# The input projection of a hybrid encoder layer: pairs of blocks by Strassen's seven products

## The chip, the cores and the metric

The kernel runs on one core of one Trainium2 chip. The metric is the device time of one execution in microseconds (us); lower is better. A core has five engines that work side by side, each through its own instructions in the order in which they are written: TensorE (PE, matmuls and weight loads), VectorE (DVE), ScalarE (ACT), GpSimd (POOL) and SyncE (SP, which here issues DMAs). Matmuls add up in PSUM, eight banks of 128 x 512 fp32; everything else lies in SBUF or in DRAM.

## The reference

One layer for 768 tokens (512 of a prompt, 256 of a sample) of width 2048, in fp32. The input projection is the largest product, and the change is made to it:

```python
hn = rmsnorm(h, norm_g[i])
proj = hn @ w_in[i]                      # (768, 2048) @ (2048, 10240)
s_x, s_z, q, k, v, a_z, g_s, g_a = jnp.split(proj, cuts, axis=-1)
# widths 1024, 1024, 1024, 1024, 1024, 1024, 2048, 2048
y = s5_direction(u, ..., False) + s5_direction(u, ..., True) + ssm_d * u      # u is s_x in 64 groups of 16
y = gelu(y); y = y * sigmoid(y @ glu_w + glu_b); y = y * silu(s_z); y_s = y @ w_branch_s
o = diff_attention(q, k, v, rel_bias, lam)                                    # 4 heads, two softmaxes each
y_a = (rmsnorm(o, subln_g) * (1 - lam_init) * silu(a_z)) @ w_branch_a
merged = sigmoid(g_s) * y_s + sigmoid(g_a) * y_a
h = h + merged @ w_out                   # then the per-layer input's gate (2048 x 2048) and the last norm
```

## The kernel before

**Products.** Every fp32 operand of a large product is split in two parts (`split`, L93): ACT copies it to the high part, DVE subtracts that to get the low part. A product is then three matmuls: low by high, high by low, high by high. `Feat` (L211) makes 128 output columns feature-major: 128 x 128 weights are stationary, 384 tokens move, and the two token halves have a bank each. With K = 2048 a block has 16 k-tiles, so 16 x 3 x 2 = 96 matmuls of 384 columns, and its weights come in two pieces of 128 x 1024. `Tok` (L263) makes v token-major with 256 moving columns. Of `w_in`, 72 blocks go through `Feat`: 8 for s_x, 8 each for s_z, q, k and a_z, 16 each for the gates g_s and g_a.

**Weights.** `wload` (L180) loads piece after piece by SP into three buffers, `wsplit` (L189) splits each two pieces ahead; `ahead` (L1395) calls both. The accumulators rotate over four banks in this phase, two for each block, so a block's sums have the time of the next block to leave them; the other four banks are the side work's.

**Order.** `run_blocks` (L1402) walks the pieces, each in two halves of 24 matmuls. A half is a slot: `slot_e` (L105) first issues stores that have come due (`later`, L102) and lets each side lane issue its next piece for ACT, DVE and DMA; after the half's matmuls `slot_p` (L114) lets it issue matmuls. The side work is a queue of generators, which yield twice for each slot. The blocks come as: the projection of p while x comes in (`x_gen`, L346, splits x times the norm's gain); s_x, s_z, a_z, g_s, eleven blocks of g_a; then for each head v, k, q; the last five blocks of g_a. Beside them runs `s5_all` (L875): parameters, then for each half of the groups (`s5_half`, L597) nine batches of the inputs in five slots each, a scan over chunks (L795), four DVE operations a step and three steps a slot, and nine slots of outputs; then the gelu in nine slots. `attention` (L997) runs beside the next head's blocks. `drain` (L1435) runs what the lanes still hold when the blocks are done.

**Results.** `ev_silu` (L408) and `ev_gate` (L417) multiply by the norm's scale R, apply the sigmoid and store to DRAM; k, q and v (`ev_qk`, L956; `ev_v`, L949) go split into the attention's tiles. `y_prep` (L1133) loads and splits y for the GLU in four slots; `o_prep` (L1194), `ev_ds` (L1211) and `ev_da` (L1225) use what was stored.

## Time and profile before

| | us |
|---|---|
| median of 3 runs (lowest, highest) | 2488.8 (2487.98, 2488.87) |
| span of the profiled execution | 2485.5 |
| PE busy, weight loads | 2451.7, 2426.7 |
| DVE, ACT, POOL busy | 1139.0, 735.1, 68.0 |

The profile is taken in one execution; its span runs from the first to the last instruction, and the median of the runs is 3.3 us above it. The page's first part gives the busy time of each engine, the windows give the same by stage with the granted TensorE clock (1.00 is full speed), the groups by form give the mean time of one instruction of one shape, and the waits tell which engine stood idle until what. The mean of a matmul in the groups contains the wait for the one ahead of it, so the time of one is read from a long row of them in the chain.

### The profile page before, as it was taken

Reading aid. Unit: us, or ns where it says so; the run is one execution under the profiler, and the core shown is the slowest. Engines: PE = TensorE matmul, PEld = TensorE weight load, DVE = VectorE, ACT = ScalarE, POOL = GpSimd, SP = SyncE. Lnnn points to the kernel's source line nnn. Section 1 sums busy time; section 2 is a strip of 40 time slices with the busy share of each in tenths; the row PEclk is TensorE's granted clock in tenths of the full one; section 3 lists DMA queues with packets and bytes.
Section 4 is the critical chain, followed back from the end, with each engine's and each line's share of the span. In section 5 each row is a group of like instructions: output and inputs, shape, how many; then the busy total and the mean of one; then the engine's idle time right before and its main releaser. Section 6 shows DMA issues by size and latency. Waiting matters only on the chain.

```text
span 2485.5 us, 35850 instructions
## 1 busy us (share of the span) xinstructions
PE 2451.7 (99%) x14902; PEld 2426.7 (98%) x14902; DVE 1139.0 (46%) x2281; ACT 735.1 (30%) x1300; POOL 68.0 (3%) x58
## 2 busy tenths in 40 slices
PE   7999999999999999999999999999999999999997
PEld 7999999999999999999999999999999999999986
DVE  8645648535556627123343434452345232253346
ACT  5223321323231233123232323431123221133233
POOL 5000000000000000000000000000000000000003
PEclk9999999999999999999999999999999999999998
DMA  7262322473222467222222122553332322222234
GB/s 293 85 157 96 110 85 87 140 158 112 92 94 94 120 173 271 79 60 64 68 65 69 56 72 73 196 182 111 104 119 98 93 86 92 80 89 86 82 115 163
DMA packets 118051, 277.93 MB, mean 112 GB/s; under 512 B 28864, under 2 KB 47040, under 8 KB 117888
## 3 DMA queue, kind: packets, MB, share of 16 engines
q1 hardware_dynamic: 117312, 274.59, 35.5%
q8 instruction: 117, 1.92, 0.3%
q10 hardware_dynamic: 576, 1.05, 0.1%
q14 instruction: 46, 0.38, 0.0%
HBM read 216.94 MB, written 58.65 MB: 111 GB/s over the span
## 4 chain that ended last, share of the span: by engine, by line
PE 96%; DVE 1%; issue 1%; DMA 1%; POOL 1%; ACT 0%; SPq 0%; POOLq 0%; ACTq 0%; DVEq 0%
PE acc L83 88%; PE yps L83 2%; PE o L83 1%; PE vps L83 1%; PE s L83 1%; PE kps L83 1%; POOL y L1343 1%; DVE a L80 1%; PE wps L763 1%; DMA xr<-in_xT 1%; PE wt L1053 0%; PE bb L83 0%; DVE wl L72 0%; PE ot L1086 0%; DVE pps L389 0%
## 5 line engine op out<-in xcount | busy, mean ns | idle before, releaser
L83 PE MATMUL acc<-a,wh 128*128 128x384 f32 (+2 forms) x6912 | 1486.9, 335 | 0.0
L83 PEld LDWEIGHTS acc<-a,wh 128*128 128x128 f32 x6912 | 1224.4, 188 | 4.9
L83 PE MATMUL acc<-a,wl 128*128 128x384 f32 (+2 forms) x3456 | 898.4, 337 | 9.3 <-DVE wl L72 6.5
L83 PEld LDWEIGHTS acc<-a,wl 128*128 128x128 f32 x3456 | 619.4, 188 | 15.8 <-DVE wl L72 6.7
L72 DVE TENSOR_TENSOR wl<-raw,wh 128x1024 fp32r<-128x1024 f32 (+1 forms) x279 | 344.9, 1237 | 607.7 <-ACT wh L69 606.5
L69 ACT ACTIVATE wh<-raw 128x1024 fp32r<-128x1024 f32 (+1 forms) x279 | 292.7, 1051 | 605.9 <-PE acc L83 335.3
L83 PE MATMUL acc<-y,wh 128*128 128x384 f32 (+2 forms) x1024 | 222.6, 336 | 0.0
L72 DVE TENSOR_TENSOR stg<-acc,R 128x384 f32<-128x384 f32 (+2 forms) x160 | 86.4, 583 | 254.8 <-PE acc L83 254.7
L83 PEld LDWEIGHTS acc<-y,wh 128*128 128x128 f32 x1024 | 181.6, 189 | 1.8
L83 PE MATMUL acc<-wh,a 128*128 128x256 f32 x768 | 139.0, 283 | 0.0
L83 PE MATMUL acc<-y,wl 128*128 128x384 f32 (+2 forms) x512 | 134.0, 336 | 0.0
L83 PEld LDWEIGHTS acc<-wh,a 128*128 128x128 f32 x768 | 119.5, 191 | 0.3
L69 ACT ACTIVATE stg<-stg 128x384 f32<-128x384 f32 (+3 forms) x91 | 46.9, 542 | 240.7 <-DVE stg L72 240.7
L83 PE MATMUL acc<-wl,a 128*128 128x256 f32 x384 | 109.1, 284 | 0.0
L83 PEld LDWEIGHTS acc<-y,wl 128*128 128x128 f32 x512 | 93.3, 189 | 0.9
L69 ACT ACTIVATE stg<-y 128x384 f32<-128x384 f32 (+2 forms) x64 | 32.0, 525 | 160.2 <-DVE y L72 160.2
L83 PEld LDWEIGHTS acc<-wl,a 128*128 128x128 f32 x384 | 73.5, 191 | 0.2
L72 DVE TENSOR_TENSOR y<-acc,stg 128x384 f32<-128x384 f32 x32 | 16.4, 553 | 86.8 <-PE acc L83 86.8
L72 DVE TENSOR_TENSOR a<-acc,stg 128x384 f32<-128x384 f32 x32 | 16.4, 553 | 82.8 <-PE acc L83 82.8
L148 POOL TENSOR_TENSOR ors<-rsm,mhalf 128x1 f32<-128x1 f32 x24 | 13.0, 543 | 1487.5 <-DVE rsm L77 1487.5
L69 ACT ACTIVATE a<-stg 128x384 fp32r<-128x384 f32 (+1 forms) x48 | 26.2, 577 | 84.4 <-DVE stg L72 76.8
L69 ACT ACTIVATE st<-vps 64x252 f32<-64x252 f32 (+1 forms) x128 | 41.1, 321 | 20.8 <-PE vps L83 18.3
(223 smaller groups left out, 1730.2 us busy)
## 6 DMA issues: line engine op xcount, KB each, us to landing
raw<-in_w_in SPq DMA_DIRECT2D x144, 512.0 KB, 3.7
raw<-in_ple_g_w SPq DMA_DIRECT2D x42, 512.0 KB, 3.6
raw<-in_w_out SPq DMA_DIRECT2D x32, 512.0 KB, 3.6
d_q<-q SPq DMA_DIRECT2D x16, 512.0 KB, 3.8
q<-d_q SPq DMA_DIRECT2D x16, 512.0 KB, 3.8
raw<-in_w_v SPq DMA_DIRECT2D x16, 512.0 KB, 3.7
raw<-in_w_s SPq DMA_DIRECT2D x16, 512.0 KB, 3.7
raw<-in_w_a SPq DMA_DIRECT2D x16, 512.0 KB, 3.6
```

Of the source, the lines that this page charges most:

```text
L69: return nc.scalar.activation(out=out, in_=in_, func=func, **kw)
L72: return nc.vector.tensor_tensor(out=out, in0=a, in1=b, op=op)
L80: return nc.vector.scalar_tensor_tensor(out=out, in0=a, scalar=s, in1=b, op0=op0, op1=op1)
L83: return nc.tensor.matmul(out, lhsT, rhs, start=start, stop=stop, **kw)
L148: nc.gpsimd.tensor_tensor(out=out, in0=m, in1=mhalf[:, :ss.shape[1]], op=ALU.pow)
L763: nc.tensor.transpose(wps[x][:, g * 128:(g + 1) * 128], w[:, x, g], ident)
L1343: (nc.gpsimd if b % 3 else nc.vector).tensor_tensor(out=h, in0=h, in1=rb, op=M)
```

## The change

62 of the 64 blocks of s_z, q, k, a_z, g_s and g_a are taken in 31 pairs. K is gone through twice: first its rows 0 to 1023 for all pairs, then the others. Within a half of K the pair of blocks, the two quarters of K and the two token halves form a 2 x 2 by 2 x 2 product, made with seven products of 12 matmuls (4 k-tiles, 3 each) in place of eight (Strassen's scheme, in Winograd's form). Sums of weight tiles are made by DVE and split for each pair and half (`step`); sums of token tiles once for each half of K (`t_prep`, from x loaded again). The seven products go to three of four banks, and a bank is copied out by ACT or added by DVE one product later (`events`). Results of the first half are stored to DRAM without norm or activation; those of the second half are added there by a DMA of POOL's queue with `accum_op`. Two blocks of g_a go plainly, in parts of half of K, between the passes.

What follows from it elsewhere: the norm's scale and the activations come where the stored rows are used (gelu, `o_prep`, `ld_gate`, attention); v, k, q pass through DRAM and `attention` loads and splits them (21 slots a head, 18 before); s_x is stored in the order in which the groups are read; half the copies of the states for the outputs move from DVE to ACT; x's second half of K is loaded again between the passes; y is loaded and split at the last pair; silu and sigmoid are no longer applied on the way out.

```diff
+    def store(dst, st, add):
+        if add:
+            nc.gpsimd.dma_start(out=dst, in_=st, accum_op=A_)
+        else:
+            dma(dst, st)
+    class Quad:
...
+        def step(self, n, j):
+            r1, r2 = raws[j], raws[j + 1] if j + 1 in raws else None
+            lo, hi = slice(0, 512), slice(512, 1024)
...
+            if n == 0:
+                h, l = wtile("wh"), wtile("wl")
+                split(h, l, r1)
+                w["a11"], w["a12"] = (h[:, lo], l[:, lo]), (h[:, hi], l[:, hi])
+            elif n == 1:
+                u = wtile("wa", qpool["p"])
+                split(u[:, lo], u[:, hi], r2[:, hi])
+                w["a22"] = u[:, lo], u[:, hi]
+                tt(r2[:, hi], r2[:, lo], r2[:, hi], A_)
+            elif n == 2:
+                tt(r2[:, lo], r2[:, lo], r1[:, lo], A_)
+                tt(r1[:, lo], r1[:, lo], r2[:, hi], A_)
+            elif n == 3:
+                h, l = wtile("wh"), wtile("wl")
+                split(h, l, r2)
+                w["s3"], w["s1"] = (h[:, lo], l[:, lo]), (h[:, hi], l[:, hi])
+            elif n == 4:
+                u = wtile("wh")
+                split(u[:, lo], u[:, hi], r1[:, lo])
+                w["s2"] = u[:, lo], u[:, hi]
+            elif n == 5:
+                tt(r1[:, hi], r1[:, lo], r1[:, hi], A_)
+                u = wtile("wl")
+                split(u[:, lo], u[:, hi], r1[:, hi])
+                w["s4"] = u[:, lo], u[:, hi]
+                raws.pop(j), raws.pop(j + 1)
...
+        def product(self, n):
...
+            acc, wn, mov, k0, cols, first = ((self.A, "a11", None, 0, t1, 1), (self.B, "a12", None, 4, t1, 1),
+                                             (self.A, "s2", "u", 0, t1, 0), (self.C, "s3", "v", 0, t2, 1),
+                                             (self.A, "s1", "u", 0, t2, 0), (self.C, "a22", "v", 0, t1, 0),
+                                             (self.A, "s4", None, 4, t2, 0))[n]
...
+            if n == 0:
+                def f():
+                    self.o1 = stg()
+                    act(self.o1[:, lo], self.A)
+                e(1, f)
+            elif n == 1:
+                e(1, lambda: tt(self.o1[:, lo], self.o1[:, lo], self.B, A_))
+            elif n == 2:
+                def f():
+                    self.o2 = stg()
+                    act(self.o2[:, lo], self.A)
+                e(1, f)
+            elif n == 3:
+                e(1, lambda: act(self.o1[:, hi], self.C))
+            elif n == 4:
+                e(1, lambda: act(self.o2[:, hi], self.A))
+            elif n == 5:
+                def f():
+                    tt(self.o2[:, hi], self.o1[:, hi], self.o2[:, hi], S_)
+                    tt(self.o2[:, lo], self.C, self.o2[:, lo], S_)
+                e(1, f)
+                e(2, lambda: store(self.dsts[1], self.o2, self.half))
+            else:
+                e(1, lambda: act(self.o1[:, hi], self.A))
+                e(2, lambda: store(self.dsts[0], self.o1, self.half))
...
+    def t_prep(p):
...
+            if i < 4:
+                tt(b[:, HT:], a[:, HT:], b[:, HT:], S_)
+                tt(a[:, HT:], a[:, :HT], a[:, HT:], S_)
+                tt(a[:, :HT], b[:, HT:], a[:, :HT], S_)
+                tt(b[:, :HT], b[:, :HT], a[:, :HT], A_)
...
-                        nc.vector.tensor_copy(out=sb[64:128, :, x, c0:c0 + n], in_=v[64:128, :, ::-1])
+                        act(sb[64:128, :, x, c0:c0 + n], v[64:128, :, ::-1])
...
+                tt(z, z, R, M)
+                act(p, z, AF.Sigmoid)
                 tt(z, z, yn, M)
+                tt(z, z, p, M)
...
     def attention(h):
...
+        open_att()
+        vr = atile("vr", (128, NT, 256), F32)
+        dma(vr.rearrange("p t e -> p (t e)"), dv[h])
...
+        ld("k", dk)
...
+        vh, vl = atile("vh", (128, NT, 256)), atile("vl", (128, NT, 256))
+        split(vh, vl, vr)
...
+                if n == "q":
+                    stt(f, f, 128.0 ** -0.5, R, M, M)
+                else:
+                    tt(f, f, R, M)
+                split(hi, l, f)
...
     def run_blocks(lo, hi):
...
+            if isinstance(blk, Quad):
+                nxt = pieces[j + 2][0] if quad_of(j + 2) else None
+                blk.begin()
+                for n in range(7):
+                    prod[0] += 1
+                    hook(j, n)
+                    run_events()
+                    if n == 0:
+                        for k in range(blk.ready, 6):
+                            blk.step(k, j)
+                    elif n in (1, 6):
+                        if n == 6 and nxt:
+                            nxt.step(4, j + 2)
+                        more()
+                    elif nxt:
+                        nxt.step(n - 2, j + 2)
+                    elif n in (2, 5):
+                        wsplit(j + 2 + (n == 5))
+                    if prod[0] % 2 == 0:
+                        slot_e()
+                    blk.product(n)
+                    if prod[0] % 2 == 1:
+                        slot_p()
...
+    hooks[j - 2, 5] = [y_load]
+    hooks[j - 2, 6] = [lambda: y_split(range(4))]
+    hooks[j, 0] = [lambda: y_split(range(4, 8))]
```

## Rows read from the trace of the kernel before

**Rows 1.** The page's first part: busy us (share of the span) xinstructions.
```profile
PE 2451.7 (99%) x14902; PEld 2426.7 (98%) x14902; DVE 1139.0 (46%) x2281; ACT 735.1 (30%) x1300; POOL 68.0 (3%) x58
```

**Rows 2.** Windows: stretch, length, busy us (xcount) of PE, PEld, DVE, ACT, POOL, clock, DMA, GB/s.
```profile
16.00:60.00 44.00, 36.18 (x193) 34.81 (x192) 44.00 (x41) 26.60 (x39) 29.14 (x14) 0.96 0.75 278
367.50:471.50 104.00, 104.00 (x603) 104.00 (x602) 82.78 (x297) 22.02 (x33) 0.00 (x0) 1.00 0.33 105
755.00:859.00 104.00, 104.00 (x603) 104.00 (x602) 74.92 (x283) 20.21 (x30) 0.00 (x0) 1.00 0.35 101
921.50:960.00 38.50, 38.50 (x224) 38.50 (x223) 27.11 (x29) 15.63 (x20) 0.00 (x0) 1.00 0.73 252
1595.50:2080.00 484.50, 484.50 (x2797) 484.37 (x2796) 190.36 (x276) 115.05 (x160) 0.00 (x0) 1.00 0.36 120
```

**Rows 3.** The chain in order of time, 1600 to 1700 us: start, us, what, xcount.
```profile
1599.94 100.19 PE acc L83 x578
```

**Rows 4.** Waits, 14 to 64 us: who waited for whom, us, times, longest.
```profile
PE acc L83 <- DVE pps L389: 7.8, 4, 2.6
```

**Rows 5.** Groups by form, whole span: instruction, shapes, xcount, busy us, mean ns, idle before.
```profile
L72 DVE TENSOR_TENSOR wl<-raw,wh 128x1024 fp32r<-128x1024 f32 x277 | 343.5, 1241 | 604.7 <-ACT wh L69 603.5 <-DMA tp<-d_z 1.2
...
L72 DVE TENSOR_TENSOR w<-t,t 128x512 f32<-128x512 f32 x32 | 22.1, 692 | 1.1
...
L72 DVE TENSOR_TENSOR stg<-stg 128x384 f32<-128x384 f32 x38 | 19.5, 554 | 18.3 <-ACT stg L69 18.3
...
L72 DVE TENSOR_TENSOR y<-y,y 128x768 fp32r<-128x768 f32 x8 | 7.7, 959 | 7.3 <-ACT y L69 7.3
...
L69 ACT ACTIVATE wh<-raw 128x1024 fp32r<-128x1024 f32 x277 | 291.5, 1054 | 604.8 <-PE acc L83 335.3 <-issue 268.0 <-DMA raw<-in_ple_p 1.1
...
L69 ACT ACTIVATE stg<-y 128x512 f32<-128x512 f32 x5 | 3.2, 632 | 7.4 <-DVE y L72 7.4
...
L69 ACT ACTIVATE pps<-acc 128x384 f32<-128x384 f32 x16 | 7.2, 480 | 0.9 <-PE acc L83 0.9
...
L69 ACT ACTIVATE y<-y 128x768 fp32r<-128x768 f32 x8 | 6.8, 847 | 17.3 <-DVE y L72 17.3
```

**Rows 6.** Groups by form, DVE, the first scan's window, 367.5 to 471.5 us.
```profile
L72 DVE TENSOR_TENSOR st<-s,s 128x128 f32<-128x128 f32 x31 | 9.1, 292 | 1.1
...
L72 DVE TENSOR_TENSOR s<-s,st 128x128 f32<-128x128 f32 x31 | 8.8, 284 | 0.0
L72 DVE TENSOR_TENSOR st<-s,s 128x64 f32<-128x64 f32 x32 | 7.2, 225 | 1.1
...
L72 DVE TENSOR_TENSOR s<-s,st 128x64 f32<-128x64 f32 x32 | 7.0, 218 | 0.0
```

**Rows 7.** Groups by form, whole span: the gelu's DVE operations.
```profile
L72 DVE TENSOR_TENSOR yn<-y,p 128x768 f32<-128x768 f32 x8 | 14.1, 1768 | 0.0
...
L77 DVE TENSOR_SCALAR p<-p 128x768 f32<-128x768 f32 x8 | 4.4, 556 | 3.6 <-ACT p L69 3.5
```

**Rows 8.** DMA issues: out, in, queue, xcount, KB of one, median us to landing.
```profile
xr<-in_xT SPq DMA_DIRECT2D x8, 768.0 KB, 8.1
...
d_gs<-stg SPq DMA_DIRECT2D x16, 384.0 KB, 2.3
...
d_ysz<-z SPq DMA_DIRECT2D x8, 384.0 KB, 4.9
...
stg<-d_y SPq DMA_DIRECT2D x8, 384.0 KB, 3.6
```

**Rows 9.** Groups by form, whole span: ACT's copies of the states for the outputs.
```profile
L69 ACT ACTIVATE sb<-st 64x256 f32<-64x256 f32 x32 | 19.3, 653 | 0.0
...
L69 ACT ACTIVATE sb<-st 64x128 f32<-64x128 f32 x32 | 11.9, 420 | 0.0
```

**Rows 10.** Groups by form, 16 to 60 us: a busy POOL, and DVE beside it.
```profile
L356 POOL TENSOR_TENSOR sqa<-sqa,sq 128x768 f32<-128x768 f32 x7 | 17.9, 2550 | 0.6
...
L72 DVE TENSOR_TENSOR wl<-raw,wh 128x1024 fp32r<-128x1024 f32 x4 | 6.4, 1602 | 0.0
```

More of the change, by code (lines that the diff above doesn't have):

```diff
@@ L263, in _build, with __init__ @@
     class Tok:
-        def __init__(self, wname, first, xs, evac):
-            self.pieces = [d[wname][first + i] for i in range(4)]
-            self.xs, self.evac = xs, evac
+        def __init__(self, wname, first, xs, evac, order=(0, 1, 2, 3)):
+            self.pieces = [d[wname][first + i] for i in order]
+            self.xs, self.evac, self.order = xs, evac, order
             self.pre = self.post = None
@@ new lines, in _build, with __init__, begin, mms @@
+    class Part:
+        def __init__(self, wname, blk, half, xs, dst):
+            self.pieces = [d[wname][blk * 2 + half]]
+            self.half, self.xs, self.dst = half, xs, dst
+            self.pre = self.post = None
+            self.wait = 0
+        def begin(self):
+            self.acc = [bank(b, "acc")[:, :HT] for b in next_banks(2)]
+        def mms(self, pi, sub, wh, wl):
+            xh, xl = self.xs
+            for kk in range(4 * sub, 4 * sub + 4):
+                k = 8 * self.half + kk
+                w = slice(kk * 128, kk * 128 + 128)
+                for i, (ww, xx) in enumerate(((wl, xh), (wh, xl), (wh, xh))):
+                    for acc, (lo, hi) in zip(self.acc, HALVES):
+                        mm(acc, ww[:, w], xx[k][:, lo:hi], start=(kk == 0 and i == 0), stop=(kk == 7 and i == 2))
+        def end(self):
+            st = stg()
+            act(st[:, :HT], self.acc[0])
+            nc.vector.tensor_copy(out=st[:, HT:], in_=self.acc[1])
+            later(lambda: store(self.dst, st, self.half))
@@ L444, in _build, with ev_v, f, put @@
-    end_b1 = len(blocks)
+    def ev_v(h):
+        def f(it):
+            st = [stg(), stg()]
+            v = [s.rearrange("p (t e) -> p t e", t=3) for s in st]
+            for t, acc in it:
+                o = v[t // 3][:, t % 3]
+                if t % 2:
+                    ts(o, acc, rs_x[:, t:t + 1])
+                else:
+                    act(o, acc, AF.Copy, scale=rs_x[:, t:t + 1])
+            def put():
+                for i in range(2):
+                    dma(dv[h][:, i * T:(i + 1) * T], st[i])
+            later(put)
+        return f
@@ new lines, in _build, with rows @@
+    for h in range(4):
+        blocks.append(Tok("w_v", 4 * h, hx, ev_v(h), (2, 3, 0, 1) if h == 3 else (0, 1, 2, 3)))
+    end_v = len(blocks)
+    def rows(blk):
+        for dst, first, n in ((dsz, SZ, 8), (dqq, Q_, 8), (dk, K_, 8), (daz, AZ, 8), (dgs, GS, 16), (dga, GA, 16)):
+            if first <= blk < first + n:
+                return dst[(blk - first) * 128:(blk - first + 1) * 128, :]
+    pairs = [(SZ + 2 * i, SZ + 2 * i + 1) for i in range(4)]
+    for h in range(4):
+        pairs += [(K_ + 2 * h, K_ + 2 * h + 1), (Q_ + 2 * h, Q_ + 2 * h + 1)]
@@ new lines, in _build @@
+    pairs += [(AZ + 2 * i, AZ + 2 * i + 1) for i in range(4)]
+    pairs += [(GS + 2 * i, GS + 2 * i + 1) for i in range(8)]
+    pairs += [(GA + 2 * i, GA + 2 * i + 1) for i in range(7)]
+    PLAIN = (GA + 14, GA + 15)
+    for half in range(2):
+        if half:
+            for b in PLAIN:
+                blocks.append(Part("w_in", b, 0, hx, rows(b)))
+            last_k0 = len(blocks) - 1
+            for b in PLAIN:
+                blocks.append(Part("w_in", b, 1, hx, rows(b)))
+        for n, p in enumerate(pairs):
+            q = Quad("w_in", p, half, hx, tx, [rows(b) for b in p])
+            if half and n == 3:
+                q.post = lambda: later(lambda: done.add("sz"), 3)
+            if half and p[0] in range(Q_, Q_ + 8, 2):
+                q.post = lambda h=(p[0] - Q_) // 2: later(lambda: lane.add(attention(h)), 3)
+            blocks.append(q)
@@ L447, in _build @@
+    end_b2 = len(blocks)
     s5c = {}
@@ L1414, in run_blocks @@
             for sub in range(2):
+                prod[0] += 2
+                run_events()
+                hook(j, sub)
+                if quad_of(j + 1):
+                    for k in (2 * sub, 2 * sub + 1):
+                        pieces[j + 1][0].step(k, j + 1)
                 slot_e()
```

325 lines of the change are left out of this document (202 added, 123 removed).

## The prediction

> **What bounds the kernel now.** The busy times come first: PE 2451.7 of 2485.5 us, DVE 1139.0, ACT 735.1 [rows 1]. PE is the bound over the whole span, but a mean says nothing of a stage, so the second view is the windows by stage [rows 2]. From 1595.5 to 2080 PE has no idle time and DVE is busy 39%; the chain of waits agrees, 578 matmuls of 384 columns in a row in 100.19 us [rows 3], 173.3 ns each. In two stages DVE is near its own limit: during the state scan it is busy 82.78 of 104 us with PE still full, and from 16 to 60 it is busy 44.00 of 44.00 us while PE has only 36.18 [rows 2]. There the matmuls wait 7.8 us for DVE's copies out of PSUM [rows 4]. The reader should take two things from this: removed matmuls are worth their full 173.3 ns wherever PE is the limit, and where DVE is full, PE goes at DVE's pace.
>
> **What is removed.** A pair of blocks over half of K takes 2 blocks x 8 k-tiles x 3 products of parts x 2 token halves = 96 matmuls before, and 7 x 4 x 3 = 84 of the same width after. So 62 halves of pairs save 62 x 12 = 744 matmuls, 744 x 173.3 ns = 128.9 us. Bank changes and weight loads don't alter this: there is one weight load for each matmul before and after. One of the seven products is 12 matmuls, 2.08 us; a pair-half 14.56 us; a slot of the side work is two products, 4.16 us.
>
> **What is added beside it.** By the written steps each pair-half needs on DVE two low parts of 1024 columns (1.241 us), seven operations of 512 (0.692) and three of 384 (0.554), in all 8.99 us, 2.57 us for each slot; on ACT two of 1024 (1.054), three of 512 (0.632) and five copies of 384 out of PSUM (0.480), 6.40 us, 1.83 for each slot [rows 5]. Against 14.56 us of PE both fit, if nothing else is queued. But the side work is paced by the same slots. I counted the yields of its generators: the first scan runs in slots 74 to 95, at the first pairs; the second batch of state inputs in 106 to 152, the second scan in 153 to 174, the gelu in 205 to 216, the four heads of attention from 220 on; the last product is in slot 297.
>
> **Stretch 1 and 2, the scans.** A scan is 31 steps of four operations between 0.284 and 0.292 us and 32 steps of four between 0.218 and 0.225 [rows 6], 64.1 us, over 21 slots. Beside it, the pairs put 21 x 2.57 = 54.0 us on DVE, together 118.1 us, where PE needs 21 x 4.16 = 87.4. The excess is 30.7 us for each scan. Before, the same scan left room since a block's sums had a whole block (16.6 us) to leave their banks and weights were split two pieces ahead.
>
> **Stretch 3, the gelu.** A block of it takes on DVE 0.556, the strided product 1.768 [rows 7], and now four operations of 768 columns at 0.959 [rows 5] where it had two (the norm's scale, and two factors where silu's product had been stored): 6.16 us, for eight blocks 49.3. Nine slots of pairs add 23.1: 72.4 against 37.4 us of PE, 35.0 too much.
>
> Together 96.4 us. DVE may be late by what lies between the making of a weight sum and its use: the sum of step 4 is made in the seventh product and used in the third of the next pair, two products, 4.2 us; I take that off twice, for the second scan and the gelu (the first scan begins with DVE already late, below). Step 5 makes DVE wait for ACT's 0.632 us in the middle; over the 14.6 pairs of the 51 slots that is 9.2 us. **The stretches cost 97 us** (85 to 110).
>
> **The turns between stages.** (a) Into the pairs: in the last four slots of v and the first two products, DVE has the token sums (four rounds of four operations of 384 columns and two of 768, 16.6 us [rows 5]), the first pair's steps (7.3) and the state inputs (twelve operations like the 0.692 row in five slots, 1.7 for each slot without their small ones, 7), 31 us, where PE has some 24: from one scan's start to the next are 387.5 us [rows 2] and 79 slots, 4.9 us each, and two products. With the wait for 3.1 MB of x I take 8 us (0 to 12). (b) Between the halves of K, eight slots (33.3 us) hold 16.6 us of token sums, eight low parts of x (0.959 each, 7.7), 7.2 us for the four plain parts and 5.2 of steps, 37 us, and 16 tiles of 384 KB come in first, 6.3 MB, 25 us at the 252 GB/s of the gelu window [rows 2]; the second x tiles are loaded only when stage buffers come free. I take 10 us (4 to 16). (c) At the end y is loaded only when the sixth product of the last pair has let go of its tiles: 3.1 MB, 12.5 us at that rate and 3.6 to the first landing [rows 8], and the fourth head has seven slots left over when the last product ends (304 needed, 297 there), whose softmax, transposes and norms then run one behind the other beside nothing. I take 13 us (5 to 20).
>
> **Attention.** v, k and q no longer pass from PSUM into the head: they come back from DRAM, and their loads are issued one slot (4.2 us) before their use. 768 KB of v and 384 KB for each k land in 3.6 to 8.1 us [rows 8]; then v's low part (1.8 us on DVE, half as much again as a 1024-column one) and, for each of k and q, two rounds of 0.959, 0.847 on ACT and 0.959 again [rows 5], each behind the other; q's tiles reuse k's buffers, so q's load waits for them, and the weight loads behind it on SP's queue wait too. ACT's copies out of PSUM are behind all this in ACT's order, and the same bank's next product waits for them after one product (2.08 us). I take 7 us a head, 28 in all (12 to 40). In the softmax slots ACT waits for DVE's row maxima behind a step's sums; in the second batch of state inputs DVE is at 2.57 + 1.7 us and small operations in a slot of 4.9; in the outputs' slots ACT gets eight copies of 0.653 and 0.42 us where it had four [rows 9]. These may be hidden by PE's own side products or cost up to 45 us; I take 12.
>
> **The accumulating stores.** 64 stores of the second half add in DRAM from POOL's queue. No row shows such a store. POOL is 3% busy [rows 1], so its own time is hidden; plain stores of this size land in 2.3 to 4.9 us [rows 8], while a stage buffer is wanted again some 15 us later. Taken: nothing; bounds 0 to 37 us, since DVE's operations with two inputs in SBUF run slower beside a busy POOL: the 1024-column low part takes 1.602 us from 16 to 60 [rows 10] against 1.241 in the mean [rows 5], and 64 stores that each held POOL as long as its longest operation, 2.55 us [rows 10], would stretch 126 us of DVE's work to 163.
> The Trainium skill (SBUF — State Buffer, Who interferes with whom) says that a VectorE instruction with two SBUF inputs contends with a GpSimd instruction that reads SBUF, not with one that only writes it. The rows agree for POOL's tensor operations; if describing a DMA only writes, the sum stays at what I forecast, and if it reads, the rival below holds; no run here shows which.
>
> **The sum.** 2485.5 - 128.9 + 97 + 8 + 10 + 13 + 28 + 12 = 2524.6 us for a profiled execution; the median of the runs lies 3.3 us above its span, so 2528.
>
> **Rivals.** First, not slower: only the arithmetic excess is paid. The waits of the turns, of attention and of the loads hide in the lead that the weights have, so that they cost their least, 21 us, and the stretches 85: 2488.8 - 128.9 + 106 = 2466. For it: PE bore 82.78 of 104 us of DVE without a wait [rows 2], and over the whole span DVE would be busy only 61% (1139.0 + 62 x 8.99 - 124 x 1.241 for the old low parts = 1542 of 2528 us). Against it: that was with a whole block's room for each bank, here it is one product, and from 16 to 60 PE lost time at once. It decides when all that lies outside the three stretches costs under 44 us. If the stretches too were half hidden it would be 2429. Second, the stores: if POOL's work slows DVE the time is 2528 + 37 = 2565; if a store held its stage buffer 17 us and not 15, up to 2 us in each of the 31 pairs of the second half, 2590. Third, PE's clock: from 16 to 60, with PE idle for 18%, the granted clock is 0.96 of full speed in the mean [rows 2], so a little of it at the lower level, 1.2 GHz. If the clock fell for most of both scans, a pair would take 29.1 us there in place of DVE's 19.7, 12 x 9.4 = 113 us more: 2641.
> The Trainium skill (TensorE: Matmul & The Clock Gate, HAM oscillation — how this bites in real kernels) says that PE falls to half clock when it idles too long between bursts. In the row above the loss is a few hundredths, with waits of at most 2.6 us [rows 4], and the gaps here are shorter, so the rule gets 5%.
>
> **How the numbers follow.** Chances: the forecast's case 0.48, the first rival 0.25, a draw between the two (other costs near 44 us) 0.05, the stores 0.17, the clock 0.05. The likeliest gives 2528, with bounds of its own terms from 2480 to 2585. The range leaves out the clock and the best part of the first rival: 2445 to 2605. A difference under 0.2% (5 us) can't be told from none: faster 0.25, same 0.05, slower 0.70.
>
> **What would show it.** Right: 5208 matmuls in the pairs at 173 ns; PE's busy share well under 99%, with its idle time in the windows of the two scans and the gelu, where DVE is busy over 90%; waits of PE for ACT's copies of sums and DVE's low parts; small idle pieces at the start of each head, and one of 10 us or more before the GLU. Wrong: PE full in the scans' windows (then the lead is longer than I think), or idle time spread evenly over the pairs of the second half alone (then it is the stores), or a granted clock far below 1 in the stretches.

## The result and the profile after

| | before | after |
|---|---|---|
| median of the runs (lowest, highest), us | 2488.84 (2487.98, 2489.82) | 2613.89 (2612.83, 2618.26) |
| span of the profiled execution, us | 2485.5 | 2612.6 |
| mean granted clock of PE | 0.995 | 0.958 |

The changed kernel takes 1.0505 times as long (95% interval 1.049 to 1.052). The direction was forecast, the size was not: 2614 lies 86 us above 2528 and 9 above the range. From the page: busy time of each engine, the granted clock in 40 slices, and POOL's DMA queue with the accumulating stores. The first line answers to [rows 1].

```profile
PE 2420.5 (93%) x14158; PEld 2371.2 (91%) x14158; DVE 1519.3 (58%) x2793; ACT 1035.4 (40%) x1837; POOL 124.8 (5%) x122
...
PEclk9999999979999998997999999989999999999998
...
q0 software_dynamic: 9216, 25.17, 6.3%
```

The 744 matmuls are gone and would have made PE 128.9 us less busy, 2322.8. It is busy 2420.5, so 97.7 us came back in matmuls that each took longer. PE is idle 192.1 us where it was idle 33.8, 158.3 more. 97.7 + 158.3 - 128.9 = 127.1 us, the whole difference of the spans. The forecast had 168 us of waits and nothing for the matmuls' length.

The stages, from the windows (columns as in [rows 2]; the decimal after POOL's time is the granted clock). They are, in order: the turn into the pairs, the first scan, its outputs, the second state inputs, the second scan, its outputs, the turn between the halves of K, five undisturbed pairs, the gelu, attention to the fourth head's start, the rest of the pairs, and all from the GLU on.

```profile
377.00:390.00 13.00, 11.97 (x59) 11.65 (x60) 10.33 (x17) 7.36 (x16) 0.00 (x0) 0.87 0.43 152
390.00:503.00 113.00, 98.06 (x526) 96.14 (x525) 101.98 (x325) 37.62 (x62) 0.00 (x0) 0.94 0.35 116
503.00:607.00 104.00, 86.87 (x454) 84.79 (x453) 28.54 (x43) 56.50 (x112) 0.00 (x0) 0.82 0.45 130
607.00:848.00 241.00, 232.95 (x1447) 229.70 (x1446) 184.71 (x321) 116.64 (x246) 0.00 (x0) 1.00 0.39 134
848.00:957.00 109.00, 93.37 (x504) 91.45 (x502) 98.74 (x315) 35.70 (x59) 0.00 (x0) 0.95 0.34 113
957.00:1026.00 69.00, 55.92 (x289) 54.39 (x289) 13.88 (x19) 39.26 (x77) 0.00 (x0) 0.80 0.44 126
1026.00:1087.00 61.00, 45.80 (x242) 42.62 (x241) 32.62 (x44) 35.64 (x55) 1.07 (x1) 0.86 0.66 203
1087.00:1160.00 73.00, 72.66 (x419) 72.66 (x420) 43.45 (x62) 30.84 (x51) 7.80 (x9) 1.00 0.59 142
1160.00:1245.00 85.00, 54.66 (x257) 52.10 (x256) 71.33 (x84) 37.62 (x55) 5.25 (x6) 0.82 0.65 195
1245.00:1600.00 355.00, 333.12 (x1913) 323.43 (x1912) 234.95 (x449) 177.00 (x377) 43.29 (x56) 0.96 0.53 126
1600.00:1715.00 115.00, 96.89 (x536) 92.59 (x535) 68.65 (x132) 54.94 (x117) 12.48 (x17) 0.90 0.55 139
1715.00:2612.00 897.00, 879.58 (x5059) 868.82 (x5058) 408.19 (x572) 270.31 (x381) 20.85 (x13) 0.99 0.34 111
```

A useful reading of such a row is its length less PE's busy time times the granted clock: full-speed time that was lost, by waiting (length less busy) or by the clock (busy times what is missing to 1). In the first outputs that is 104 - 86.87 x 0.82 = 32.8 us, 17.1 of them waits and 15.6 clock. The split is an estimate, since the clock is the mean over the whole row, waits included. Summed in the forecast's terms (its 12 also held the softmax slots, which lie in the attention row here):

| stage | forecast, us | lost after, us | of it by the clock |
|---|---|---|---|
| turn into the pairs | 8 | 3 | 2 |
| two scans | 65 | 41 | 11 |
| outputs and state inputs (the "12") | 12 | 65 | 27 |
| turn between the halves | 10 | 22 | 6 |
| gelu | 32 | 40 | 10 |
| attention and the end | 41 | 63 | 23 |
| sum | 168 | 234 | 79 |

Before, PE was full here (two windows of that trace):

```profile
400.00:1200.00 800.00, 799.47 (x5063) 797.43 (x5062) 389.48 (x950) 233.00 (x449) 2.20 (x4) 1.00 0.40 119
1200.00:1589.00 389.00, 389.00 (x2506) 384.81 (x2505) 140.86 (x316) 126.13 (x270) 10.84 (x20) 1.00 0.24 74
```

The sum should be 127.1 + 128.9 = 256; the clock is given in hundredths, which over 1182 us of busy PE leaves up to 6 us either way, and the other 16 or so are not placed. The waits of these rows add to 155 us, close to the 158 of the page, so what is missing lies in time in which PE is busy. From the GLU on nothing changed (897 us, 896 before), and the five undisturbed pairs of the second half took 14.6 us each, as forecast.

The outputs' slots are thus the term that was missed, and they look like this (PE, then ACT, from their timelines; start, length, instruction, in brackets the idle time ahead of it):

```profile
528.09 0.58 PE L91 MATMUL yps<-u,tp 128*128 128x96 f32 x4
531.07 2.04 PE L91 MATMUL yps<-sb,q 128*128 128x96 f32 x8 [2.41 <-ACT sb L77]
...
538.84 2.24 PE L91 MATMUL acc<-a,wa 128*128 128x384 f32 x12
540.92 0.58 PE L91 MATMUL yps<-u,tp 128*128 128x96 f32 x4
544.46 0.69 PE L91 MATMUL yps<-sb,q 128*128 128x96 f32 x4 [2.95 <-ACT sb L77]
...
526.20 0.49 ACT L77 ACTIVATE stg<-acc 128x384 f32<-128x384 f32 x1 [4.75 <-PE acc L91]
526.59 0.62 ACT L77 ACTIVATE wa<-raw 128x512 fp32r<-128x512 f32 x1
527.11 0.54 ACT L77 ACTIVATE y<-yps 128x192 f32<-128x192 f32 x2
527.53 4.36 ACT L77 ACTIVATE sb<-st 64x256 f32<-64x256 f32 x8
```

ACT waits for a product's end, then does its copy, a split, the last outputs' copies and eight state copies (4.36 us); PE does one product in that time and then waits for the copies. Reading the code with this in hand gives the reason. The products are counted on from pair to pair; `slot_e` is called ahead of each even one and `slot_p` behind each odd one. The first pair begins on an odd product, so `slot_p` is called first and takes the lane's ACT/DVE part, and `slot_e`, next in line and ahead of the next product, takes its PE part; the order stays so in the pairs that follow. No product lies between a part for ACT and the matmuls that need it. The forecast had counted slots but not in which of the two calls each part goes out.

### The profile page after: what moved, and what is told of

It is laid out like the page before. It is cut to its first block, busy times and chain, and to the rows that moved or that the text cites. A ratio compares the mean times of both kernels' runs of the same rounds, so it can differ in the third digit from the quotient of the medians.

```text
span 2612.6 us, 36211 instructions
## 1 busy us (share of the span) xinstructions
PE 2420.5 (93%) x14158; PEld 2371.2 (91%) x14158; DVE 1519.3 (58%) x2793; ACT 1035.4 (40%) x1837; POOL 124.8 (5%) x122
## 4 chain that ended last, share of the span: by engine, by line
PE 44%; issue 6%; DVE 6%; ACT 4%; DMA 2%; POOL 1%; SPq 0%; POOLq 0%; ACTq 0%; DVEq 0%
PE acc L91 42%; DVE wl L80 1%; ACT wh L77 1%; ACT stg L77 1%; POOL y L1595 1%; DVE z L80 1%; DVE stg L80 1%; DVE yn L80 1%; DVE a L80 0%; ACT p L77 0%; PE yps L91 0%; DVE p L80 0%; PE o L91 0%; DMA stg<-in_xT 0%; DVE raw L80 0%
## 5 line engine op out<-in xcount | busy, mean ns | idle before, releaser
L91 PE MATMUL acc<-a,wh 128*128 128x384 f32 (+2 forms) x5672 | 1309.8, 342 | 52.5 <-ACT stg L77 50.2
L91 PEld LDWEIGHTS acc<-a,wh 128*128 128x128 f32 x5672 | 1036.3, 193 | 66.5 <-ACT stg L77 58.0
L77 ACT ACTIVATE stg<-acc 128x384 f32<-128x384 f32 x314 | 151.7, 487 | 335.7 <-PE acc L91 256.0
L91 PE MATMUL acc<-a,wa 128*128 128x384 f32 x744 | 150.1, 352 | 21.5 <-ACT stg L77 21.5
L91 PEld LDWEIGHTS acc<-a,wa 128*128 128x128 f32 x744 | 137.8, 200 | 23.7 <-ACT stg L77 23.7
L77 ACT ACTIVATE stg<-stg 128x768 f32<-128x768 f32 (+3 forms) x64 | 43.2, 686 | 173.8 <-DVE stg L80 173.8
L80 DVE TENSOR_TENSOR raw<-raw,raw 128x512 f32<-128x512 f32 x124 | 85.7, 691 | 3.5
L80 DVE TENSOR_TENSOR raw<-raw 128x512 f32<-128x512 f32 x124 | 85.3, 688 | 2.1
L80 DVE TENSOR_TENSOR wl<-raw,wl 128x512 fp32r<-128x512 f32 x62 | 43.0, 693 | 65.8 <-ACT wl L77 65.8
L91 PE MATMUL yps<-sb,q 128*128 128x96 f32 x256 | 53.8, 370 | 29.5 <-ACT sb L77 29.5
```

What stands on the lines that cost most here:

```text
L77: return nc.scalar.activation(out=out, in_=in_, func=func, **kw)
L80: return nc.vector.tensor_tensor(out=out, in0=a, in1=b, op=op)
L91: return nc.tensor.matmul(out, lhsT, rhs, start=start, stop=stop, **kw)
```

## Experiments

Each is the changed kernel with one edit unless said otherwise; before took 2488.7 to 2490.0 us in each comparison. The pairs' times below are from one accumulating matmul to the same one of the next pair; 84 matmuls at 173.3 ns are 14.56 us.

**The side work in step.** A lane keeps its own phase:

```diff
     def adv(self, part):
+        if part != self.ph:
+            return
         while self.q:
             try:
                 next(self.q[0])
+                self.ph = "P" if part == "E" else "E"
                 return
...
```

> The changed kernel, with the side work put back in step: a lane gives out a part for ACT and DVE only ahead of a slot's first product and a part for PE only behind its second, so two products lie between the copies and the matmuls that use them. The phase theory (in the pairs the copies are issued with no product between them and their matmuls, PE stands idle, and the clock falls with it): each of the two outputs' stretches goes from some 104 and 110 us to 72 to 80, 60 us off the total, 2545 to 2560 us, and the granted clock in them returns to over 0.95. ACT's load alone (eight copies are too many for a slot, whatever the order): at most 15 us off, 2600. Clock alone (the level falls of itself): no change, 2614. The forecast on record has no term for it and gives 2614 too.

2563.17 us, ratio 1.0295 (1.0278 to 1.0312): 51 us off. The pairs of the first half take 598 us instead of 648, those of the second 616 instead of 627, while the turn between them takes 10 more. PE's wait for the state copies falls from 17.1 us in the first outputs to 1.5:

```profile
PE yps L91 <- ACT sb L77: 17.1, 11, 3.0
...
PE yps L96 <- ACT sb L82: 1.5, 3, 1.1
```

The first line is of the changed kernel, the second of this one (total, times, longest). The two outputs' stretches of this kernel, the second up to the turn:

```profile
488.60:566.80 78.20, 70.31 (x421) 68.75 (x419) 35.98 (x82) 52.03 (x100) 0.00 (x0) 0.91 0.52 154
924.50:976.80 52.30, 45.22 (x289) 44.01 (x288) 19.39 (x44) 35.79 (x69) 0.00 (x0) 0.94 0.58 175
```

The phase theory holds, with two misses: the time is 3 us above its range, and the clock came back to 0.91 and 0.94, not to over 0.95.

**Half of the copies on VectorE.**

```diff
-                        act(sb[64:128, :, x, c0:c0 + n], v[64:128, :, ::-1])
+                        nc.vector.tensor_copy(out=sb[64:128, :, x, c0:c0 + n], in_=v[64:128, :, ::-1])
```

> The changed kernel with half of the state copies of the outputs' slots on VectorE and half on ScalarE, so that the chain ahead of the matmuls is shorter by about half of 4.4 us. The order of the parts is left as it is. Phase theory: 2 us of each of 16 slots and some of the clock's loss, 35 to 50 us off, 2565 to 2580. ACT's load alone: 60 us off or more, 2550, since ACT has then what it had before the change. Clock alone: 2614.

2570.28 us, ratio 1.0326 (1.031 to 1.0341): 44 us off, inside the phase theory's range and short of the 60 that ACT's load alone would give. Both edits shorten the same chain.

**PE kept busy in the outputs.**

```diff
+                fill = hh[7] if hh[15] is first15 else hh[15]
+                for _ in range(20):
+                    mm(yps[1][:, 256:512], fill[:, :128], fill[:, :256], True, True)
```

> The changed kernel, the order of its side work as it is, with 20 matmuls of 256 columns that nothing reads ahead of each of the 16 groups of output matmuls, some 2.1 us at full clock, where PE now waits 2.4 to 3.0 us for ScalarE's copies. Theory that the idle time takes the clock along, and the clock costs more than the waits: PE then stays near full clock in both stretches (0.82 and 0.80 before), the products and output matmuls, 66 us of work at full clock against 87 busy in the first stretch, come out that much shorter, and the total falls by 20 to 35 us, 2580 to 2594, though work was added. Theory that the clock falls there of another cause (the short 4-byte matmuls themselves): the clock stays at 0.8 and the total is the same or up to 17 us longer, 2614 to 2631.

2589.38 us, ratio 1.0406 (1.0389 to 1.0424): 24.5 us off, with 320 matmuls more. The two outputs' stretches (the row of the first in the changed kernel, 503 to 607, holds one undisturbed pair more), and what PE still waited for in the first:

```profile
503.00:578.00 75.00, 72.80 (x523) 70.86 (x523) 20.73 (x30) 50.47 (x100) 0.00 (x0) 1.00 0.55 162
938.00:1006.00 68.00, 63.16 (x434) 61.68 (x433) 20.63 (x40) 40.71 (x79) 0.00 (x0) 0.97 0.53 154
...
PE yps L91 <- ACT sb L77: 1.9, 8, 0.7
```

The clock stays at 1.00 and 0.97 (0.82 and 0.80 before the edit). So it was the idle time ahead of the output matmuls, in pieces of at most 3.0 us, that took the clock down, and the clock's part of the outputs' loss is real time.
The Trainium skill (TensorE: Matmul & The Clock Gate, HAM oscillation — how this bites in real kernels) describes PE falling to half clock when it idles too long between bursts. The direction is what these rows show; the prediction put the gaps here below what matters, and that was the error.

**The clock in the gelu.** 12 such matmuls ahead of each product there.

```diff
+            if fill[0]:
+                fb, fx = bank(7, "fill"), hh[15]
+                for _ in range(fill[0]):
+                    mm(fb[:, :256], fx[:, :128], fx[:, :256], True, True)
```

> The changed kernel with 12 matmuls of 256 columns that nothing reads, some 1.3 us at full clock, ahead of each product of the gelu's slots, where PE is idle 1.4 us for each. The granted clock there should rise from 0.82 to over 0.95. If VectorE and ScalarE set the pace there, the clock costs nothing and the three pairs stay at 84 us: 2609 to 2619. If the clock adds to their time as it did in the outputs' slots: 8 to 15 us off, 2599 to 2606.

2618.36 us, ratio 1.0523 (1.0508 to 1.0539), no shorter. The clock rose only from 0.82 to 0.90, and the three pairs took 88 us against 84.5:

```profile
1161.00:1246.00 85.00, 74.05 (x451) 73.17 (x451) 70.38 (x82) 36.91 (x54) 5.24 (x6) 0.90 0.62 186
```

In the changed kernel PE waited there only eight times:

```profile
PE acc L91 <- ACT stg L77: 30.3, 8, 10.3
```

The added matmuls stand ahead of 18 products, so they also took time where PE had nothing to wait for. That the higher clock gave nothing back because VectorE and ScalarE set the pace is likely, but this run does not separate it from the time of the added matmuls. So of the 79 us in the table's last column, some 24 of the outputs' 27 are shown to be time; for the gelu's 10 that is not shown.

**A third of the scan.**

```diff
         for m in range(1, 64):
+            if m % 3:
+                continue
```

> The changed kernel with only every third of the 63 steps of each state scan, in the same slots; the other steps are left out. The theory that VectorE bounds the scans: its work for a slot goes from 3.05 + 2.57 us to 1.02 + 2.57 us, under the 4.16 us of the two products, so both scans go at the pace of the products and the whole excess of 47 us that the trace shows there goes, 2567. If the stretch is bound by something else (the turn into the pairs, waits for weights, the clock): less than 20 us off, 2594 or more.

2565.04 us, ratio 1.0305 (1.0289 to 1.032): 49 us off, and PE is full in the scans:

```profile
395.00:468.00 73.00, 73.00 (x423) 73.00 (x422) 55.93 (x132) 30.38 (x50) 0.00 (x0) 1.00 0.44 147
846.00:919.00 73.00, 70.83 (x413) 70.50 (x412) 51.48 (x118) 32.69 (x55) 0.00 (x0) 0.99 0.45 146
```

The scans are bound by VectorE, as forecast.

**One of VectorE's six operations in the gelu.**

```diff
-                ts(p, p, 0.044715, 1.0, M, A_)
-                tt(p, p, y, M)
...
-                tt(z, z, R, M)
...
-                tt(z, z, yn, M)
-                tt(z, z, p, M)
```

> The changed kernel with one of VectorE's six operations in each block of the gelu, the strided product (the polynomial, the gate's scale and its two products are left out). VectorE's work for a slot goes from 6.16 + 2.57 us to 1.77 + 2.57 us, next to the 4.16 us of the products. Theory that VectorE alone bounds the gelu: its three pairs go from 84.5 us to 44 to 50, 35 to 41 us off, 2573 to 2579. If ScalarE, the loads of y and z or the clock bound it as well: under 20 us off, 2594 or more.

2590.36 us, ratio 1.0408 (1.0392 to 1.0423): 23.5 us off, between the two expectations. With VectorE at half its load the three pairs still take 62 us, not 44, and what PE waits for is ScalarE's copy of a product (the row holds one undisturbed pair more):

```profile
1160.00:1240.00 80.00, 68.61 (x357) 66.69 (x356) 50.42 (x65) 45.54 (x68) 7.75 (x9) 0.91 0.86 258
...
PE acc L91 <- ACT stg L77: 11.4, 6, 5.0
```

That copy stands behind a sigmoid that waits for VectorE. So VectorE's amount of work is somewhat over half of the gelu's loss; that the rest is the order between the two engines is read from these waits and was not tested by itself.

**Attention's inputs earlier.** The next head's v and k are loaded before the head ends, q into v's buffer.

```diff
-            if n == "k":
-                ld("q", dqq)
...
+            if u == NT - 1 and h < 3:
+                nv = vr_of(h + 1)
+            if u == NT and h < 3:
+                att_in[h + 1] = nv, k_of(h + 1)
```

> The changed kernel with attention's inputs loaded earlier: the next head's v two softmax steps, its k one step before the head ends, and q into v's buffer as soon as v is split, not into k's buffers behind k. Theory of the forecast's term (the loads' landing in the head's first slots costs 7 us a head): the pair at each head's start goes from 27 to some 20 us, 20 to 28 us off, 2586 to 2594. If it is the order of the copies out of PSUM behind the splits on ScalarE and VectorE: under 8 us off, 2606 or more.

2613.28 us, ratio 1.0497 (1.0481 to 1.0513): nothing. The pair at a head's start still takes 26 to 27 us. The forecast's reason for that term was wrong.

**The same work in stages.**

```diff
-        split(vh, vl, vr)
+        act(vh, vr)
...
+            for f, hi, l in t3:
                 if n == "q":
                     stt(f, f, 128.0 ** -0.5, R, M, M)
                 else:
                     tt(f, f, R, M)
-                split(hi, l, f)
+            for f, hi, l in t3:
+                act(hi, f)
+            if n == "k":
+                tt(vl, vr, vh.bitcast(F32), S_)
+            for f, hi, l in t3:
+                tt(l, f, hi.bitcast(F32), S_)
```

> The changed kernel with the operations on attention's k and q tiles in stages (both scales, then both high parts, then both low parts, v's low part after k's high parts) where each tile's three went one behind the other. The work is the same. If attention's first slots are held by the chain in order between VectorE and ScalarE, behind which the products' copies stand: 4 to 6 us a head, 16 to 24 us off, 2590 to 2598. If VectorE's amount of work holds them: 0 to 5 us off, 2609 or more.

2593.46 us, ratio 1.0419 (1.0401 to 1.0436): 20 us off with the same instructions. ScalarE's timeline at the second head, of the changed kernel and then of this one:

```profile
1379.26 1.48 ACT L77 ACTIVATE vh<-vr 128x1536 fp32r<-128x1536 f32 x1
1383.44 0.85 ACT L77 ACTIVATE kh<-p 128x768 fp32r<-128x768 f32 x1 [2.69 <-DVE p L80]
1386.17 0.84 ACT L77 ACTIVATE kh<-p 128x768 fp32r<-128x768 f32 x1 [1.89 <-DVE p L80]
1386.92 1.04 ACT L77 ACTIVATE wh<-raw 128x1024 fp32r<-128x1024 f32 x1
1387.87 0.47 ACT L77 ACTIVATE stg<-acc 128x384 f32<-128x384 f32 x1
...
1376.75 1.49 ACT L77 ACTIVATE vh<-vr 128x1536 fp32r<-128x1536 f32 x1
1378.12 1.57 ACT L77 ACTIVATE kh<-p 128x768 fp32r<-128x768 f32 x2
1379.59 1.05 ACT L77 ACTIVATE wh<-raw 128x1024 fp32r<-128x1024 f32 x1
1380.54 0.48 ACT L77 ACTIVATE stg<-acc 128x384 f32<-128x384 f32 x1
```

The copy of a product (the last line of each) comes 8.6 us after v's high part began, and 3.8 us in the staged kernel. In between ScalarE stood idle 4.6 us, for VectorE's scale of each tile, and VectorE in turn waited for ScalarE's high part.

**Without VectorE's part of that preparation.**

```diff
-        split(vh, vl, vr)
+        vh = atile("vh", (128, NT, 256))
+        act(vh, vr)
+        vl = vh
...
-                if n == "q":
-                    stt(f, f, 128.0 ** -0.5, R, M, M)
-                else:
-                    tt(f, f, R, M)
-                split(hi, l, f)
-                to.append((hi, l))
...
+                act(hi, f)
+                to.append((hi, hi))
```

> The changed kernel without VectorE's nine operations at each head's start (scales and low parts of v, k and q are left out; ScalarE's high parts stay and stand for both). It prices the whole of that preparation: if attention's loss is there, the pair at each head's start goes from 27 to 17 us or less, 40 to 48 us off, 2566 to 2574. If it is spread over the softmax slots: under 20 us off, 2594 or more.

2579.95 us, ratio 1.0367 (1.0351 to 1.0382): 34 us off, below the 40 expected; the pair at a head's start takes 17.6 to 19.7 us. The staged order alone gave 20 of these 34.

**Plain stores in place of accumulating ones.**

```diff
-            nc.gpsimd.dma_start(out=dst, in_=st, accum_op=A_)
+            dma(dst, st)
```

> The changed kernel with the second half's 64 stores as plain ones from the sync queue, so the first half of K is not added in the stored blocks. The rival of the accumulating stores: 37 us off or more, 2577 and less. If they cost nothing, as the sum has it: within 5 us of 2614.

2609.7 us, ratio 1.0486 (1.0471 to 1.0502): the interval overlaps the changed kernel's, so the accumulating stores cost at most a few us. The rival of the stores is out.

**The weight sums on GpSimd.**

```diff
+    def ptt(out, a, b, op):
+        return nc.gpsimd.tensor_tensor(out=out, in0=a, in1=b, op=op)
...
-                tt(r2[:, hi], r2[:, lo], r2[:, hi], A_)
+                ptt(r2[:, hi], r2[:, lo], r2[:, hi], A_)
...
-                tt(r2[:, lo], r2[:, lo], r1[:, lo], A_)
-                tt(r1[:, lo], r1[:, lo], r2[:, hi], A_)
+                ptt(r2[:, lo], r2[:, lo], r1[:, lo], A_)
+                ptt(r1[:, lo], r1[:, lo], r2[:, hi], A_)
...
-                tt(r1[:, hi], r1[:, lo], r1[:, hi], A_)
+                ptt(r1[:, hi], r1[:, lo], r1[:, hi], A_)
```

> The changed kernel with the four weight sums of each step list (512 columns each) on GpSimd instead of VectorE. If GpSimd's tensor operations cost VectorE nothing: VectorE's work for a slot of the pairs goes from 2.57 to 1.78 us, the two scans lose 31 less 14 us each at most, some 20 to 30 us together, the gelu 7: 2580 to 2594. If the two slow each other as from 16 to 60 us in the kernel before (1.602 against 1.241 us for one low part), GpSimd is busy for a third of the time and nothing is gained, and late sums are waited for: 2614 to 2650.

2659.14 us, ratio 1.0678 (1.066 to 1.0696): 45 us more and 9 above the second expectation, though VectorE has 248 operations less. A group of the first scan's steps on VectorE, in the changed kernel and in this one (count, busy, mean ns), and GpSimd's sums:

```profile
L80 DVE TENSOR_TENSOR s<-st,a8i 128x128 f32<-128x128 f32 x28 | 8.0, 284 | 0.0
...
L80 DVE TENSOR_TENSOR s<-st,a8i 128x128 f32<-128x128 f32 x29 | 11.6, 399 | 0.0
...
L88 POOL TENSOR_TENSOR raw<-raw 128x512 f32<-128x512 f32 x124 | 187.1, 1509 | 1058.7 <-DVE wa L80 962.1 <-DVE r L1305 49.5 <-DMA d_yr<-y 23.4
```

A step's operation goes from 284 to 399 ns in the mean beside GpSimd's reads: 26 of the 29 take as long as before (279 to 289 ns), and three take 1.4 us. The Trainium skill (SBUF — State Buffer, Who interferes with whom) says that a VectorE instruction with two SBUF inputs contends with a GpSimd instruction that reads SBUF. These rows agree. Describing a DMA is not such a reader here: in the changed kernel, from 1080 to 1715 us, VectorE's sums of 512 columns take 684 ns while GpSimd issues an accumulating store (23 of them) and 691 ns otherwise (39).

The longer operations are not shown to be what costs the 45 us. The five whole pairs of the first scan take 93.7 us here and 94.0 in the changed kernel; some 26 of the 45 us come in attention's pairs, where ScalarE now waits for the sums themselves (1.51 and 1.42 us each on GpSimd, 0.69 on VectorE). The first line is of the changed kernel, 1260 to 1690 us, the second of this one, 1260 to 1730 us:

```profile
ACT wl L77 <- DVE raw L80: 5.3, 11, 1.0
...
ACT wl L77 <- POOL raw L88: 26.6, 19, 2.5
```

**The second half's x from GpSimd's queue.**

```diff
-                dma(raw[i][x], d["xT"][:, 8 * p + 4 * x + i])
+                (nc.gpsimd if p else nc.sync).dma_start(out=raw[i][x], in_=d["xT"][:, 8 * p + 4 * x + i])
...
-                dma(raw[k], d["xT"][:, 8 + k])
+                nc.gpsimd.dma_start(out=raw[k], in_=d["xT"][:, 8 + k])
```

> The changed kernel with the 16 loads of the second half's x from GpSimd's queue, so that they don't stand behind the outputs' stores and loads on the sync queue. Theory that this queue, not the bandwidth, holds the turn between the halves: the four plain parts go from 61 us to 42 to 48, 13 to 19 us off, 2595 to 2601. Bandwidth or VectorE's token sums: under 5 us off, 2609 or more.

2615.51 us, ratio 1.0504 (1.0488 to 1.0519): nothing, so the sync queue does not hold the turn between the halves.

**All pairs plain.** The two passes and all that goes with them, without the seven products.

```diff
-            q = Quad("w_in", p, half, hx, tx, [rows(b) for b in p])
+            for b in p:
+                q = Part("w_in", b, half, hx, rows(b))
...
-    hooks[start_of[end_v] - 2, 0] = [lambda: lane2.add(t_prep(0))]
...
-    hooks[j - 1, 0] = [lambda: lane2.add(t_prep(1))]
```

> The changed kernel with every pair as two plain blocks over half of K (eight products for seven): two passes, sums added in DRAM, v, k and q through DRAM and the loads of x and y as in the changed kernel, but no token sums and no steps of pairs. The forecast's terms for what is left come to 51 us (between the halves 10, end 13, attention 28): 2540. If the seven products' own work is what costs, as the trace has it for scans and gelu, this is at or under 2545 and shows no excess in the scans. If the passes through DRAM are what costs: 2590 or more.

2541.38 us, ratio 1.021 (1.0195 to 1.0226), 1 us from the forecast's terms. A pair in either scan takes 16.6 us, its 96 matmuls, with no loss. The first outputs, the second outputs, the turn, the gelu, and a head of attention:

```profile
501.80:556.00 54.20, 50.27 (x312) 49.40 (x312) 10.82 (x21) 26.65 (x52) 0.00 (x0) 0.97 0.64 181
869.00:935.00 66.00, 61.61 (x403) 60.74 (x402) 7.14 (x8) 41.26 (x82) 0.00 (x0) 0.95 0.60 180
985.00:1024.00 39.00, 35.16 (x195) 33.16 (x194) 15.01 (x16) 13.06 (x17) 1.07 (x1) 1.00 0.57 175
1123.00:1179.00 56.00, 41.76 (x200) 39.42 (x199) 42.57 (x49) 19.76 (x26) 4.93 (x5) 0.85 0.84 242
1198.00:1315.00 117.00, 115.05 (x677) 112.68 (x676) 49.83 (x106) 42.31 (x91) 13.95 (x18) 0.99 0.49 120
```

In attention PE is idle 2 us in 117 here, with the same loads and the same preparation: a plain block's sums have a block's time to leave their banks. By these rows the outputs lose 13 us, the turn 4, the gelu 20.5 and a head 3, 50 in all with four heads, where the forecast's 51 were the turn, the end and attention: that the sum fits is luck, and half of the gelu's 40 is there without the pairs. So the two passes cost 52.5 us, and the seven products, which save 129, cost 201: 2613.9 - 2541.4 = 72.5.

The turn between the halves takes 38.8 us here, where the outputs end before it and no token sums are made; 33.3 are its matmuls.

**The seven products where there is room.** 17 pairs only, side work in step, half the copies on VectorE, the gelu over twice the slots.

```diff
+            if n in ((9, 10, 11, 12, 13, 14, 15, 16, 17, 18, 19, 20), (0, 1, 2, 3, 4))[half]:
+                q = Quad("w_in", p, half, hx, tx, [rows(b) for b in p])
+                blocks.append(q)
+            else:
+                for b in p:
+                    q = Part("w_in", b, half, hx, rows(b))
...
```

> The two passes with the seven products only where the traces show VectorE and ScalarE with room: 12 pairs of the first half beside the state inputs and the first 5 of the second half; the other 45 pairs as plain blocks. The side work is kept in step, half of the outputs' state copies are on VectorE, and a block of the gelu is spread over two slots. From 2541 us of the all-plain kernel: 17 pairs with 2.08 us each off (35), the outputs 12, the gelu 15 to 24: 2470 to 2480. If a pair brings its loss with it wherever it stands: 2500 or more.

2511.51 us, ratio 1.0088 (1.0073 to 1.0103): 30 us under the plain kernel and still slower than before. By its size this is the second expectation, but not for its reason. The pairs bring most of their 35 us (beside the second state inputs, from 550 to 775 us, PE waits 4.4 us in all), and the gelu's pairs are free of loss (16.6 us each). The outputs, of which 12 us were expected, lose as much as in the plain kernel, and the token sums, which the plain kernel doesn't have, take 22 us back: the first block pair after v takes 24.7 us instead of 16.8, and the turn between the halves 52.7 instead of 38.8.

**The repairs together.** The edits of the first two experiments and of the earlier loads, all pairs by seven products.

> The changed kernel, all 62 pairs, with the side work in step, half of the outputs' copies on VectorE, and attention's inputs loaded earlier. If the three losses are separate: 2563 (in step) less 10 and less what the earlier loads give, 2530 to 2550. If the lost time only moves on to the next in-order wait: 2555 to 2565.

2555.19 us, ratio 1.0264 (1.0249 to 1.028), 8 us under the kernel in step. The two repairs of the outputs overlap, the earlier loads give nothing, and the lost time does move on. The staged order, worth 20 us by itself, was not put together with these.

No kernel tried beats the one before.

## Why the prediction was wrong

- **Removed matmuls, 173.3 ns each:** right. Pairs without side work take 14.6 us.
- **Scans, 65 us by VectorE's sum:** right in kind, too high in size: 41 by the rows, 49 with two thirds of the steps gone. VectorE is busy there 90 and 91%, as forecast.
- **Gelu, 32:** 40. VectorE's sum was only somewhat over half of it (23.5); what is left is read as ScalarE's wait for VectorE, with a product's copy behind it, and the plain kernel loses 20.5 here too. The forecast summed each engine alone, so the near size is in part luck.
- **"In the outputs' slots ACT gets eight copies … I take 12":** this is the step that failed. The two outputs' stretches lost 57 us, and with the state inputs 65. The bound above was 45. The phase of the lane, which is in the code, was not worked out; the copies were priced as load, not as a chain with nothing beside it. Putting the lane in step gives 51 us back over the whole kernel.
- **The clock, 5%:** the second failure, and it multiplied the first. "The gaps here are shorter" was wrong: PE's waits for the copies are up to 3.0 us in the outputs, those in the gelu up to 10.3, against 2.6 in [rows 4], and those of the outputs come back in every slot. Yet the clock fell there and in the gelu (0.80 to 0.82), and far less in the scans, where the rival had put it (0.94 and 0.95); filling the outputs' gaps gives back 24.5 us.
- **Attention, 28 for its loads:** the size was nearer (35 to the fourth head's start) than the reason. Loads cost nothing; the alternation of VectorE and ScalarE that the same paragraph named, with the products' copies behind it, costs 20 to 34.
- **End, 13:** the row from 1600 to 1715 us lost 28. Its waits apart from those for products' copies are 11 us, the longest 4.5, where one idle piece of 10 us or more had been forecast.
- **Turn into the pairs, 8:** 3.
- **Turn between the halves, 10:** 22. Against the plain kernel's turn (38.8 us) and the hybrid's (52.7), the token sums are some 14 of it and the second scan's outputs, which run into it, some 9 (61.3).
- **Accumulating stores at nothing:** right.
- **Not slower:** wrong by its own condition; what lies outside the stretches cost far more than 44 us.
- **The range:** the terms' own bounds add up to 2466 and 2603 us, with the stores' 37 to 2640, not to the 2480 and 2585 that the prediction states.

What stays open: 16 us or so that the rows of windows don't place; what the lower clock costs in the gelu, in attention and the turns; and which part of the gelu's loss is order.

## What to carry to other kernels

Before an engine's work is summed over a stretch, follow one slot in the order in which it is issued: an engine at 54% can hold PE if its work starts only when PE's last product ends and the next needs it, and that order flips where a stretch begins with the other of the two calls. A scheme that saves matmuls by adding sums and copies can also leave less time to empty a bank, here one product's 2.08 us instead of the next block's 16.6; price it against the engine that empties the bank, in every stage of its side work, and use it only in those with room. Short waits that come back in every slot can cost twice, once as waits and once as clock, so a stretch that PE does not fill should be priced at both levels.

## What the chip showed that was not expected

- Waits of up to 3.0 us, 17 us in 104, take the granted clock to 0.82; the rows at the lower of its two levels are easy to see: 12 matmuls of a product took 4.21 us behind a wait of 3.67 in attention, and 2.24 at full clock, in the outputs' rows above (1.2 and 2.4 GHz):

```profile
1395.85 4.21 PE L91 MATMUL acc<-a,wa 128*128 128x384 f32 x12 [3.67 <-ACT stg L77]
```

- Matmuls that nothing reads can shorten a kernel: 320 of them took 24.5 us off.
- They need not: ahead of the products in the gelu they raised the clock from 0.82 to 0.90 and gave nothing.
- Work moved from VectorE to an idle GpSimd left most of VectorE's small operations as they were (284 ns) and held single ones for 1.4 us; the kernel became 45 us slower, 26 of them in attention's pairs, where the sums themselves came late.
